# Half of layer 1's query tiles computed in the front, two score places, conditioning sums in PSUM

## The chip, the cores and the metric

The kernel runs on one core of one Trainium2 chip. A core has TensorE (matmuls; "PE" in the profile, and "PEld" for its weight loads), VectorE (DVE), ScalarE (ACT), GpSimd (POOL) and SyncE (SP), which run side by side and wait for one another by semaphores. Data lies in SBUF (on chip), in PSUM (eight banks of 512 fp32 numbers a partition, which matmuls write) and in device memory, which DMA queues read and write; SP's queue and POOL's queue are used here. The metric is the time of one execution on the device in microseconds (us), as the median of several runs.

## What is computed

One inference step of a two-layer trunk. 512 sample tokens and 128 prompt tokens, 640 columns in all, go through the same weights with a model width of 2048, all in fp32. Each layer is: norm, a shift and scale from the conditioning vector, one wide input projection, two mixers with SiLU gates, one output projection, a gated residual. Layer 0 has windowed attention and a short convolution. Layer 1, which is changed here, has differential attention (C) and grouped attention (D):

```python
def odd_mixer(h, w_in, w_out, ...):
    cq, ck, cv, cg, dq, dk, dv, dg = split_cols(h @ w_in, ODD_SPLIT)
    cq = rms_norm(cq..., cqn);  ck = rms_norm(ck..., ckn)
    q_d = rms_norm(q_heads(dq, ...), dqn);  k_d = rms_norm(kv_heads(dk, ...), dkn)
    # samples: rotary on q and k, cached keys and values in front
    o1 = attend(cq[:, 0], ck_all[:, 0], cv_all);  o2 = attend(cq[:, 1], ck_all[:, 1], cv_all)
    o_c = rms_norm(o1 - lam * o2, c_on) * (1 - lam_init)
    y = concat(o_c * silu(cg), attend(q_d, dk_all, dv_all) * silu(dg))
    return y @ w_out
```

C has four heads with two query tiles each (one for each softmax map), D has eight heads that share two keys and are worked on in pairs. So there are 16 query tiles of 128 columns each, eight attention items (four pairs of D, four heads of C), and 52 column tiles in layer 1's input projection. The conditioning of a layer is a product of two vectors with a 2048 x 6144 matrix, in twelve blocks of 512 columns.

## The kernel before

**Numbers.** An fp32 matmul is made of three: weight and data are each split into a rounded part (ACT, line 297) and a rest (VectorE, line 298), and hi x hi, hi x lo and lo x hi are summed in PSUM. The 640 columns are taken in two halves of 320.

**Single tiles and pairs.** A column tile alone (`proj_q`, lines 325 to 334) takes 16 row blocks x 3 products x 2 halves, 96 matmuls of 320 columns. `run_pairs` (lines 534 to 645) takes two column tiles at once by a seven-product scheme in place of eight: 7 x 8 row blocks x 3 = 168 matmuls. It pays with sums on VectorE (lines 566 to 579) and after the products (lines 603 to 609), and it wants the whole of its results at once, in halves, tile by tile; the results go to the function that belongs to the tile (gate, key or value), which ends with a store to device memory.

**Stages** (by the first matmul of each, from the trace): layer 0's single tiles from 36 us, its pairs from 656, its output projection from 880; layer 1's front from 1092 with six single tiles, its 14 pairs from 1180 to 1546 (eight gates, ten keys, ten values); the odd stage from 1546, which has 18 single tiles (16 queries, two gates) with both attentions between them; layer 1's output projection from 2016, its pairs from 2114 to the end.

**The odd stage.** `run_tiles` goes through the tiles in quarters of 24 matmuls. Query tiles 0 and 1 of an item are neighbours; each goes through `q_gen` (line 742: scale and square out of PSUM, a rotary turn with a copy from SBUF to SBUF by DMA, sums of squares, splits). With the second one the item's attention is put into the list `attn`. After each half of a quarter `pace_attn` takes a number of steps of that list, 0.5 to 1 by `steps(i)`. An item has some 14 steps; a full query block of 128 tokens takes two of them (`pair_gen`, line 864; `diff_gen`, line 1554). A step computes scores into PSUM (`scores`, lines 840 to 852), takes the maximum (VectorE, line 808), the exponential (ACT, line 815), transposes the weights (PE, line 834), splits them and weighs the values (lines 897 to 899, 1605 to 1607). Scores have one place of two banks (`pS`), the single tiles have two places (`pproj`, tags pa0, pb0, pa1, pb1), and two banks (`pT`) serve transposes and the rest.

**Fills.** Conditioning blocks that are not needed yet are summed by VectorE, two operations of 512 columns for each of 16 row blocks, in between. `slot` takes steps of such a fill at a given rate. The last four blocks, 8 to 11 of layer 1 (`fill1`, `ada_on_dve`, line 192), are summed in SBUF during the odd stage, fetched by SP's queue, from the third tile on at a rate of 1.1.

**Order.** The program text sets a first order, and the framework orders each engine's instructions by it when it builds, by its own estimate of when each can start; in the trace, scores of the next step can stand amid a weighing. Each engine then works through its list in order. A tile name with `bufs=n` has n buffers, and a new one waits for the oldest to come free.

## Time and profile before

| what | before |
|---|---|
| median of 3 runs | 2251.61 us (2249.99 to 2255.14) |
| the profiled execution | 2249.84 us |
| its span, first to last instruction | 2248.0 us |
| mean granted TensorE clock | 0.998 |
| layer 1's pairs in the front, 1179.7 to 1546.3 | 366.6 us: PE busy 362.8, DVE 255.2, ACT 204.7, POOL 40.6 |
| odd stage up to 2030 | 483.7 us: PE busy 476.3, DVE 370.5, ACT 305.5, POOL 53.8 |

The profile is of one execution. "Busy" is the time in which an engine works on at least one instruction; matmuls overlap, so that a matmul is shown with some 0.31 us while the next one starts 0.15 us after it. A row of a group of instructions gives line, engine, operation, output<-inputs, shapes and count, then busy time and mean ns of one, then the idle time of the engine just before and what ended it. A timeline row begins with the start and the length. A row of waits says which engine at which line waited for which, with total, times and longest.

### The profile page before, as it was taken

To read this page: it belongs to the slowest core of one execution; us is meant where nothing else is said; L and a number is where in the kernel's file an instruction comes from. 1 tells how busy PE (TensorE), PEld (TensorE's weight loads), DVE (VectorE), ACT (ScalarE), POOL (GpSimd) and SP (SyncE) were. 2 spreads that over 40 slices of the span, in tenths; PEclk is the share of its full clock that TensorE was granted. 3 is DMA by queue.
4 is the path that set the end of the run, shared out by engine and by line. 5 is a ranking of instruction groups with operands and counts; after the bars stand their busy time and mean duration, and the time that the engine had idled before them with its cause. 6 is when DMAs were issued, how large, how long until landed. Compare 5 with 4: busy or idle time off the path is not lost.

```text
span 2248.0 us, 41180 instructions
## 1 busy us (share of the span) xinstructions
PE 2208.3 (98%) x15564; PEld 2133.0 (95%) x15564; DVE 1729.8 (77%) x3027; ACT 1131.9 (50%) x2423; POOL 230.1 (10%) x349
## 2 busy tenths in 40 slices
PE   7999999999999999999999999999999999999999
PEld 5889999999999999999999999999999998999999
DVE  5659898989888978877777677765859697976765
ACT  4335453535334445444644466545666666563443
POOL 2211001000100100000100011101000011111010
PEclk9999999999999999999999999999999999999999
DMA  9985556565444526743773333335425343556541
GB/s 357 342 281 180 173 163 209 174 195 171 146 149 122 156 88 198 228 144 121 239 227 114 108 99 105 107 121 163 131 81 162 96 144 113 162 158 228 177 133 44
DMA packets 383543, 365.84 MB, mean 163 GB/s; under 512 B 18786, under 2 KB 326464, under 8 KB 382832
## 3 DMA queue, kind: packets, MB, share of 16 engines
q1 hardware_dynamic: 365984, 300.25, 43.8%
q0 software_dynamic: 16496, 60.74, 7.5%
q8 instruction: 122, 2.00, 0.4%
q10 hardware_dynamic: 864, 2.23, 0.3%
q14 instruction: 77, 0.63, 0.1%
HBM read 310.05 MB, written 46.79 MB: 159 GB/s over the span
## 4 chain that ended last, share of the span: by engine, by line
PE 83%; DMA 5%; issue 4%; DVE 4%; ACT 3%; POOL 2%; SPq 0%; ACTq 0%; POOLq 0%; DVEq 0%
PE pq L627 11%; PE pq L628 11%; PE pq L629 11%; PE pa L332 6%; PE pa L333 6%; PE pb L332 6%; PE pa L334 6%; PE pb L333 6%; PE pb L334 6%; PE T L834 2%; PE S L846 2%; PE S L848 1%; PE S L847 1%; PE T L178 1%; PE T L897 1%
## 5 line engine op out<-in xcount | busy, mean ns | idle before, releaser
L297 ACT ACTIVATE wh<-raw 128x512 fp32r<-128x512 f32 (+1 forms) x364 | 218.5, 601 | 351.8 <-PE pb L333 229.1
L627 PE MATMUL pq<-h,wh 128*128 128x320 f32 x1088 | 338.1, 311 | 0.0
L628 PE MATMUL pq<-h,wh 128*128 128x320 f32 x1088 | 336.2, 309 | 0.0
L629 PE MATMUL pq<-h,wl 128*128 128x320 f32 x1088 | 335.9, 309 | 0.0
L332 PE MATMUL pa<-h,wh 128*128 128x320 f32 x1024 | 325.7, 318 | 0.2 <-DVE sum L426 0.2
L332 PE MATMUL pb<-h,wh 128*128 128x320 f32 x1024 | 321.0, 314 | 0.9 <-ACT h L297 0.9
L333 PE MATMUL pa<-h,wh 128*128 128x320 f32 x1024 | 319.2, 312 | 0.6 <-DVE h L298 0.6
L334 PE MATMUL pb<-h,wl 128*128 128x320 f32 x1024 | 318.5, 311 | 0.2 <-DVE wl L298 0.2
L333 PE MATMUL pb<-h,wh 128*128 128x320 f32 x1024 | 317.7, 310 | 0.0
L334 PE MATMUL pa<-h,wl 128*128 128x320 f32 x1024 | 317.4, 310 | 0.0
L298 DVE TENSOR_TENSOR wl<-raw,wh 128x512 fp32r<-128x512 f32 (+1 forms) x364 | 236.9, 652 | 92.0 <-ACT wh L297 87.9
L627 PE MATMUL pq<-T,wh 128*128 128x320 f32 x816 | 253.8, 311 | 0.0
L629 PE MATMUL pq<-T,wl 128*128 128x320 f32 x816 | 252.3, 309 | 0.1
L628 PE MATMUL pq<-T,wh 128*128 128x320 f32 x816 | 252.0, 309 | 0.0
L297 ACT ACTIVATE wh<-sx 128x512 fp32r<-128x512 f32 x204 | 127.9, 632 | 162.7 <-PE pq L628 117.6
L627 PEld LDWEIGHTS pq<-h,wh 128*128 128x128 f32 x1088 | 204.3, 188 | 0.8 <-issue 0.8
L628 PEld LDWEIGHTS pq<-h,wh 128*128 128x128 f32 x1088 | 204.4, 188 | 0.0
L332 PEld LDWEIGHTS pa<-h,wh 128*128 128x128 f32 x1024 | 192.4, 188 | 12.5 <-issue 11.6
L629 PEld LDWEIGHTS pq<-h,wl 128*128 128x128 f32 x1088 | 204.2, 188 | 0.0
L333 PEld LDWEIGHTS pa<-h,wh 128*128 128x128 f32 x1024 | 192.6, 188 | 6.0 <-issue 4.9
L332 PEld LDWEIGHTS pb<-h,wh 128*128 128x128 f32 x1024 | 193.1, 189 | 2.1 <-ACT h L297 1.1
L334 PEld LDWEIGHTS pa<-h,wl 128*128 128x128 f32 x1024 | 192.4, 188 | 1.6 <-issue 1.6
(399 smaller groups left out, 4904.5 us busy)
## 6 DMA issues: line engine op xcount, KB each, us to landing
adaw<-in_ada_w SPq DMA_DIRECT2D x80, 512.0 KB, 4.0
raw<-in_ev_w_in SPq DMA_DIRECT2D x130, 256.0 KB, 3.3
raw<-in_od_w_in SPq DMA_DIRECT2D x124, 256.0 KB, 3.3
ada<-in_ada_w SPq DMA_DIRECT2D x11, 2048.0 KB, 13.5
w<-in_od_w_in SPq DMA_DIRECT2D x42, 512.0 KB, 3.8
adaw<-in_ada_w SPq DMA_DIRECT2D x64, 256.0 KB, 2.8
w<-in_ev_w_in SPq DMA_DIRECT2D x27, 512.0 KB, 3.7
adah<-in_ada_w SPq DMA_DIRECT2D x20, 512.0 KB, 9.3
```

The lines of the kernel that those rows point to most:

```text
L178: PE.matmul(acc[32 * g:32 * g + 32, 0:wd], sT[:, kt, :], w[:, kt % m, :], start=(i < 4), stop=(i >= KT - 4), tile_position=(0, 32 * g))
L297: A.activation(hi, x, AF.Copy)
L298: V.tensor_sub(lo, x, hi)
L332: PE.matmul(ps, wh[:, i, :], hi[:, sl], start=(j == js[0] if alone else (pos == 0 and j == 0)), stop=False)
L333: PE.matmul(ps, wh[:, i, :], lo[:, sl], start=False, stop=False)
L334: PE.matmul(ps, wl[:, i, :], hi[:, sl], start=False, stop=(j == js[1] - 1 if alone else (pos == 3 and j == 3)))
L627: PE.matmul(ps, wh[:, j, :], hi, start=(first and h == 0 and j == 0), stop=False, skip_group_check=True)
L628: PE.matmul(ps, wh[:, j, :], lo, start=False, stop=False, skip_group_check=True)
L629: PE.matmul(ps, wl[:, j, :], hi, start=False, stop=(final and h == 1 and j == 3), skip_group_check=True)
L834: PE.transpose(t[:, i * P:(i + 1) * P], p, ident)
L846: PE.matmul(d, q[0][:, bs], k[0][:, ks], start=True, stop=False)
L847: PE.matmul(d, q[0][:, bs], k[1][:, ks], start=False, stop=False)
```

## The change

**Queries in the front.** The second query tile of each item (odd heads of D, the second map's tiles of C) leaves the odd stage. These eight columns stand between the keys and the values of the front, as four more pairs. Their results are copied raw to SBUF (`query_out`, buffers "xr") and stored in eight new scratch tiles `qdram` by POOL's queue. In the odd stage `q_rider` loads such a tile and its four turned pieces by SP's queue and does the rest of `q_gen`'s work from SBUF, with the gain put into the rotary operations, together with the item's first query.

**The odd stage** has ten single tiles in place of 18. `steps` is 3.1 and then 3.6 a quarter tile, taken in four parts of six matmuls, and one further step after each tile. All single tiles but the first use one PSUM place (`single`); the other place's two banks (the new pool "more") are closed and serve as a second place for scores (pool "twice"), and the two are taken in turn. Before the output projection they change back; it takes its leads from places 0 and 2.

**Conditioning.** Blocks 8 to 10 move to the front pairs: VectorE sums them in the score place of PSUM, idle there, fetched by POOL's queue into "xr" buffers. `front_rests` sets the rate: for each of two slots of a product, gates 1 at three products of seven, keys 0.5 at three, queries and values 1 at four. Block 11 is summed in the odd stage's first tiles, in buffers "P" of the softmax weights, and is finished before the first attention item begins.

**Smaller parts.** The keys' chain keeps its squares in the mask's buffer, no longer needed, in place of the score place, and stores from its first buffer; the odd stage's "rp" has three buffers for two, "kk" two for one; the heads' key and value loads are grouped a little differently.

```diff
-FILL1 = 1.1
-FILL1_FROM = 8
+FILL1 = 2.2
+    def score_place():
+        if ("twice", "at") not in pools:
+            return pS.tile([P, 1024], F32, tag="S", name="S")
+        st["turn"] = not st.get("turn")
+        return (pS if st["turn"] else pools["twice", "at"]).tile([P, 1024], F32, tag="S", name="S")
...
-    def ada_on_dve(blocks):
+    def ada_in_psum(blocks):
         for l, cb in blocks:
+            both = pS.tile([P, 1024], F32, tag="S", name="adaS")
+            acc = both[:, 0:512], both[:, 512:1024]
+            fetch = lambda kt: ada_in(xr_tile("adaw")[:, 0:512], l, cb, kt, nc.gpsimd)
+            ws = [fetch(0), fetch(1)]
+            yield
+            for kt in range(KT):
+                for _ in ada_rows(l, cb, kt, ws[0], acc):
+                    yield
...
+            acc = [xr_tile(f"acc{c}")[:, 0:512] for c in range(2)]
             for c in range(2):
+                A.copy(acc[c], both[:, c * 512:(c + 1) * 512])
...
+            ada_fold(l, cb, acc, pools["cur"], "xr", 5)
...
+                elif single:
+                    for k in range(4):
+                        proj_q(pp, parts[t], qd, qd, HV[k // 2:k // 2 + 1], js=(k % 2 * 2, k % 2 * 2 + 2), base=0)
+                        if k < 3:
+                            pace_attn(steps(i) / 4)
...
+            if single:
+                pace_attn(1.0)
...
+    def q_rider(j, tag, gain, then=None):
+        ap, (g, turned) = pools["cur"], gain
+        x = ap.tile([P, NT], F32, tag="x2", name="x2", bufs=1)
+        nc.sync.dma_start(x, qdram[j])
+        sw = ap.tile([P, NS], F32, tag="rp", name="qsw", bufs=st["rp"])
+        for d in range(4):
+            nc.sync.dma_start(sw[32 * d:32 * d + 32, :], qdram[j][32 * (d ^ 1):32 * (d ^ 1) + 32, 0:NS])
+        yield
+        sq = ap.tile([P, NT], F32, tag="stg", name="qsq", bufs=2)
+        A.activation(sq, x, AF.Square)
+        m = ap.tile([P, NS], F32, tag="rp", name="qm", bufs=st["rp"])
+        V.scalar_tensor_tensor(out=m, in0=x[:, 0:NS], scalar=g, in1=cosT, op0=ALU.mult, op1=ALU.mult)
+        V.scalar_tensor_tensor(out=sw, in0=sw, scalar=turned, in1=sinT, op0=ALU.mult, op1=ALU.mult)
+        sb = q_sums(ap, sq)
+        yield
...
     def scores(q, blk, k, segs, masks=()):
-        s = pS.tile([P, 1024], F32, tag="S", name="S")
+        s = score_place()
...
+    FRONT_COLS += [OD["dq"] + i * P for i in (1, 3, 5, 7)] + [OD["cq"] + i * P for i in (4, 5, 6, 7)]
+    FRONT_OUT += [(query_out, j) for j in range(8)]
...
+    def front_rests(p, name):
+        out = FRONT_OUT[N_FRONT + 2 * p][0]
+        if out is key_out:
+            return {"M6": 0.5, "M2": 0.5, "M4": 0.5}.get(name, 0.0)
+        return {"M6": 1.0, "M2": 1.0, "M3": 1.0, "M4": 0.0 if out is gate_out else 1.0}.get(name, 0.0)
...
     close("mid")
+    close_psum("more")
+    open_psum("twice")
     open_pool("odd")
-    st["sets"], st["rp"] = 2, 2
+    st["sets"], st["rp"] = 2, 3
+    fill1 = ada_in_rows(1, 11)
...
-    run_tiles(jobs, I["od_w_in"][0], None, fill1, FILL1, fill_from=FILL1_FROM,
-              steps=lambda i: brisk.get(i, 1.0))
+    run_tiles(jobs, I["od_w_in"][0], None, fill1, FILL1, steps=lambda i: 3.1 if i < 6 else 3.6,
+              single=lambda i: 0 if i else 2)
     drain(prep)
+    wait_for("scores", done0 + 8)
```

227 lines of the change are left out of this document (144 added, 83 removed).

## The prediction

> **What bounds the kernel now.** I read the page first: the share of each engine and the chain that ended last.
>
> ```profile
> span 2248.0 us, 41180 instructions
> PE 2208.3 (98%) x15564; PEld 2133.0 (95%) x15564; DVE 1729.8 (77%) x3027; ACT 1131.9 (50%) x2423; POOL 230.1 (10%) x349
> PE 83%; DMA 5%; issue 4%; DVE 4%; ACT 3%; POOL 2%; SPq 0%; ACTq 0%; POOLq 0%; DVEq 0%
> ```
>
> TensorE is busy for 98% of the span and makes up 83% of the chain. A busy row can hide small holes, since matmuls overlap in it, so I take matmul time from the distance of starts instead. Then I asked for the busy times by stretch. The columns are length, PE, PEld, DVE, ACT, POOL, granted clock, DMA share, GB/s.
>
> ```profile
> 730.00:880.00 150.00, 149.95 (x1026) 149.08 (x1025) 127.27 (x200) 68.91 (x121) 8.35 (x16) 1.00 0.42 128
> 1085.00:1090.00 5.00, 3.04 (x23) 2.64 (x22) 3.10 (x10) 2.66 (x6) 2.35 (x3) 1.00 0.94 333
> 1090.00:1096.00 6.00, 5.12 (x21) 4.93 (x21) 4.73 (x12) 4.80 (x14) 0.60 (x1) 0.50 0.82 282
> 1179.70:1546.30 366.60, 362.82 (x2499) 360.13 (x2498) 255.17 (x390) 204.70 (x490) 40.60 (x66) 1.00 0.35 107
> 1546.30:2030.00 483.70, 476.34 (x3334) 451.03 (x3333) 370.46 (x700) 305.54 (x691) 53.83 (x72) 1.00 0.46 139
> 1900.00:2000.00 100.00, 97.41 (x679) 92.13 (x679) 86.29 (x168) 63.31 (x156) 15.77 (x26) 1.00 0.54 163
> ```
>
> The fourth row is layer 1's front pairs, the fifth the odd stage (projections and both attentions). TensorE bounds both; VectorE has 70% and 77% of them, ScalarE 56% and 63%. Two matmuls of a pair, 55 starts apart, give the price of one 320-column matmul:
>
> ```profile
> 1535.80 0.31 PE L628 MATMUL pq<-T,wh 128*128 128x320 f32 x1
> 1543.87 0.31 PE L629 MATMUL pq<-T,wl 128*128 128x320 f32 x1
> ```
>
> 8.07 / 55 = 0.1467 us.
>
> **The change, part by part.** (1) *Eight columns of queries go from single tiles to four pairs.* A single tile is 16 row blocks x 3 products x 2 halves = 96 matmuls; a pair is 7 products x 8 x 3 = 168. Eight tiles cost 768, four pairs 672. The odd stage loses 768 x 0.1467 = 112.7 us of matmuls, the front gains 98.6 us. On the bounding engine that is 96 x 0.1467 = **-14.1 us**, all on the path as long as TensorE stays the bound in both stretches. The rest is about whether it does.
>
> (2) *The front.* What VectorE does for a pair, and what it pays for conditioning, is in the groups of instructions of the stretches 1179.7 to 1546.3 (rows one to five) and 1546.3 to 2030 (the last two):
>
> ```profile
> L298 DVE TENSOR_TENSOR wl<-sx,wh 128x512 fp32r<-128x512 f32 x83 | 56.9, 691 | 37.5 <-ACT wh L297 36.7
> L569 DVE TENSOR_TENSOR sx<-sx,w 128x1024 f32<-128x1024 f32 x14 | 17.1, 1223 | 0.3
> L566 DVE TENSOR_TENSOR sx<-w,raw 128x512 f32<-128x512 f32 x26 | 16.8, 687 | 0.3
> L609 DVE TENSOR_TENSOR tables<-pq,tables 128x320 f32<-128x320 f32 x14 | 6.9, 492 | 7.0 <-PE pq L629 7.0
> L298 DVE TENSOR_TENSOR h<-w,h 128x320 fp32r<-128x320 f32 x8 | 3.6, 487 | 0.0
> L211 DVE SCALAR_TENSOR_TENSOR acc<-adaw,sT,acc 128x512 f32<-128x512 f32 x120 | 86.1, 744 | 6.9 <-DMA adaw<-in_ada_w 6.8
> L298 DVE TENSOR_TENSOR wl<-raw,wh 128x512 fp32r<-128x512 f32 x75 | 51.6, 688 | 31.0 <-ACT wh L297 29.1 <-PE T L899 1.4
> ```
>
> A pair needs 14 splits (14 x 0.691 = 9.7), three sums of 1024 columns and two of 512 (3 x 1.223 + 2 x 0.687 = 5.0) and three of 320 (1.5): 16.2 us beside 168 x 0.1467 = 24.6 us of matmuls. Three conditioning blocks are 3 x 32 = 96 further operations of about 0.744 us, 71 us. The front becomes 366.6 + 98.6 = 465 us with 255 + 4 x 16.2 + 71 = 391 us of VectorE, 84%. Layer 0's pairs, which already carry such fills, show 127.27 of 150 us (85%) with TensorE at 149.95: no stall at that load. The only new thing is that the sums lie in PSUM, which VectorE now writes and no row shows it writing. A read from there costs 0.492 against 0.487 us (rows four and five); I take 0.75, and the ends are 0.744 (no dearer than now) and twice that. The fetches also move from SP's queue to POOL's: 48 issues, queued ahead of the keys' small powers. POOL is busy 40.6 of 366.6 us, so they fit; between nothing and the 3.8 us that TensorE is not busy in the front today (366.60 - 362.82), doubled. The stores of raw queries (eight, also POOL) and two ACT copies a tile have the same cover; the copies replace work that ACT did in the odd stage. I take +1 us, ends 0 and +4; dear PSUM writes are a rival.
>
> (3) *The second score place.* Today the next scores wait until the exponential has read the one place. That is the largest named wait of TensorE in the odd stage, first at the weight load, then at the matmul itself:
>
> ```profile
> PEld S L846 <- ACT p L815: 8.4, 30, 1.1
> PE S L846 <- ACT p L815: 1.8, 3, 0.8
> ```
>
> The weight load's wait overlaps matmuls still running, so the gain lies between -1.8 and -10.2; I take **-5 us**.
>
> (4) *Less projection beside attention.* This is the dear part. Eight items (four dense pairs, four differential heads) now share eight tiles, where they had sixteen. A stretch with little projection between shows what a step costs today; four score steps from the timeline:
>
> ```profile
> 1999.43 0.44 PE L846 MATMUL S<-k1h,q1h 128*128 128x384 f32 x1
> 2016.04 0.44 PE L846 MATMUL S<-k1h,q1h 128*128 128x384 f32 x1
> ...
> 1996.00:2016.00 20.00, 20.00 (x145) 18.88 (x144) 15.13 (x31) 13.59 (x34) 1.73 (x4) 1.00 0.19 60
> ```
>
> 16.61 / 4 = 4.15 us, and counting the timeline 37 projection matmuls stand between, 9.3 a step. After the change a quarter tile (24 matmuls) is shared by 3.1 or 3.6 steps: 7.7 or 6.7 a step. So the density is a fifth to a quarter beyond one that TensorE got through without a hole. What can open is the way from the transposes over both splits to the weighing:
>
> ```profile
> 1996.72 0.81 PE L834 MATMUL T<-ident,p 128*128 128x128 f32 x6
> 1997.35 0.60 ACT L297 ACTIVATE pth<-T 128x512 fp32r<-128x512 f32 x1
> 1997.98 1.02 DVE L298 TENSOR_TENSOR ptl<-T,pth 128x512 fp32r<-128x512 f32 x2
> 1998.84 0.28 PE L1605 MATMUL T<-vh,pth 128*128 128x256 f32 x1
> ```
>
> Projections start again at 1997.29 and the weighing at 1998.84: 1.55 us to cover, and 6.7 or 7.7 matmuls cover 0.98 or 1.13. Missing are 0.57 or 0.42 us in each of 16 + 16 full query blocks, 15.8 us in all, if nothing else stands there. Something does: in the same place the trace runs the next scores amid the weighing (weighing at 1998.84, scores at 1999.43), and with two places they can come earlier. So the ends are 0 and, where busier ACT and DVE also delay the splits, twice 15.8; I take **+6 us**, nearer to the lower end because the thin stretch above has PE busy 20.00 of 20. The engines themselves have room: VectorE 370 - 71 (three of the four blocks, 96 x 0.744) - 22 (32 splits x 0.688) = 277 of 484 - 113 = 371 us, 75%; it has 86% in 1900 to 2000 today.
>
> (5) *The opening of the odd stage.* Block 11 and four queries, keys and values now fall on the first two tiles, before attention may begin (its P places hold the sums): 32 x 0.744 = 23.8 us of fills, 11 x 0.688 = 7.6 of weight splits, two queries of three rotary operations and a split (4 x 0.686 and 0.3 for the prompt's part, 6 together) and, as an estimate, some 4 for keys and values (five splits of 640 columns or less). That is 41 us of VectorE beside 2 x 14.1 us of matmuls. Attention begins 41 us into the stage today as well, but with a third tile's matmuls before it:
>
> ```profile
> 1587.23 0.34 PE L846 MATMUL S<-k0h,q0h 128*128 128x384 f32 x1
> ...
> L762 DVE TENSOR_TENSOR qsw<-qsw,tables 128x512 f32<-128x512 f32 x16 | 11.0, 686 | 2.9 <-DMA qsw<-qx 2.8
> L298 DVE TENSOR_TENSOR h<-yin,h 128x640 fp32r<-128x640 f32 x12 | 9.7, 816 | 0.4 <-ACT h L297 0.4
> ```
>
> The hole is at most 41 - 28 = 13 us. Three quarters of the third tile (3 x 3.5 us) have their weights ordered by then and can fill it: **+3 us**, ends 0 and 13.
>
> (6) *One PSUM bank for the single tiles.* The next tile's first half waits until ACT has copied and squared it (0.52 + 0.43 us):
>
> ```profile
> L746 ACT ACTIVATE qx<-pa,vec 128x320 f32<-128x320 f32 x16 | 8.4, 524 | 9.7 <-PE pa L334 7.0 <-issue 1.5 <-DMA raw<-in_od_w_in 1.2
> L747 ACT ACTIVATE qsq<-pa 128x320 f32<-128x320 f32 x16 | 7.0, 434 | 0.0
> ```
>
> The second half's last 12 matmuls (1.76 us) and one attention step stand in between. Behind that wait in TensorE's queue is everything, so a late ACT costs in full: 0 to 9 x 1 us, **+2**.
>
> (7) *Riders.* Each rider loads its tile and four turned pieces from DRAM on SP's queue, one issue more than before, a full tile ahead of use; the DMA share is 0.46 and falls with 8 weight columns gone. Nothing, as long as that tile's 14 us cover the load. The output projection's banks change places: nothing.
>
> Sum: -14.1 + 1 - 5 + 6 + 3 + 2 = -7.1 us. The profiled execution took 2249.84 us (span 2248.0 and 1.8 around it), so 2242.7; that execution lies 1.8 below the median of the runs (2251.61), within their spread of 5. I predict **2243 us**.
>
> **The rivals.** *Thin filler (slower).* The covering scores are not there in time, because exponentials and splits queue on ACT and DVE, and every full query block opens a hole between transposes and weighing. Place: the 32 blocks of the odd stage. Price at 0.7 us each: 22 us in place of 6, so 2259. It outweighs the fewer matmuls alone from 14.1 / 32 = 0.44 us a block, and the whole sum from 13 us / 32 = 0.41. For it: 0.42 to 0.57 us are really uncovered by projections; against it: the full 20 us above. Chance 0.25.
> *Everything hides.* No hole opens, the opening is filled, score waits go: 2249.84 - 14.1 - 7 = 2229. Against it: ACT and DVE both rise to some three quarters of the stage with chains between them. Chance 0.15.
> *The front turns VectorE-bound.* At 1.49 us for a sum in PSUM, a query or value pair with eight fills needs 16.2 + 11.9 = 28.1 against 24.6 us: 9 x 3.5 = 31 us, 2274. It decides from (24.6 - 16.2) / 8 = 1.05 us an operation. Against it: 0.492 beside 0.487. Chance 0.08.
> *The opening stays a hole.* 8 us uncovered in place of 3, and the clock falls: after TensorE's gap in 1085 to 1090 the next 6 us were granted 0.50, so 3 us more: 2243 + 8 = 2251, no change. Chance 0.10. [...]
>
> **How the numbers follow.** My forecast (2236 to 2250) has 0.42, the rivals 0.25, 0.15, 0.08 and 0.10. A difference of 0.2% (4.5 us) is about what a measurement of this kernel can tell. Faster is most of my own case (0.38) and all of "everything hides": 0.53. Within 0.2%: the rest of mine, most of the opening and the mild part of thin filler: 0.18. Slower: 0.29. The range 2230 to 2264 leaves out the dear PSUM sums, the worst of thin filler and half of "everything hides", under 0.2 together.
>
> **What would show it.** Matmuls of the pair lines in the front up by 672, single ones down by 768 (1). Front near 465 us with PE busy within 5 us of it, and a fill in PSUM near 0.75 us (2). No wait of scores for the exponential (3). The odd stage's span: 371 us plus or minus few; waits of weighing or transposes for splits above 13 us in total mean thin filler (4). First scores near 41 us into the stage with TensorE holes before (5). Waits of single tiles' matmuls for ACT's square (6). I am wrong if VectorE or ACT, not TensorE, ends most waits of the odd stage, or if TensorE pauses in the front.

## The result

The changed kernel takes 2270.97 us (median of 6 runs, 2262.72 to 2276.05), the kernel before on the same chip 2252.56 (6 runs). The ratio is 1.008, with a 95% interval of 1.0067 to 1.0092: 0.8% slower, where 2243 and a range of 2230 to 2264 had been forecast. The profiled execution took 2271.45 us, 21.6 more than that of the kernel before.

The page of the changed kernel, with the span, the engines' shares and the chain that ended last:

```profile
span 2269.7 us, 41141 instructions
PE 2204.6 (97%) x15468; PEld 2118.8 (93%) x15468; DVE 1765.4 (78%) x3075; ACT 1147.2 (51%) x2457; POOL 258.3 (11%) x413
PE 79%; DVE 5%; issue 5%; DMA 5%; ACT 4%; POOL 2%; SPq 1%; POOLq 0%; DVEq 0%; ACTq 0%
```

TensorE issues 96 instructions fewer (15468 against 15564) and holds four points less of the chain, while the span grew. To see where, I cut at the first matmul of a stage. The first row is the changed kernel's front pairs, the second its odd stage with the output projection's single tiles; the columns are length, PE, PEld, DVE, ACT, POOL, granted clock, DMA share, GB/s.

```profile
1184.20:1651.40 467.20, 464.12 (x3200) 459.81 (x3200) 375.66 (x583) 253.49 (x583) 70.09 (x122) 1.00 0.43 134
1651.40:2135.50 484.10, 451.81 (x3099) 417.86 (x3098) 339.75 (x653) 303.51 (x688) 57.61 (x87) 1.00 0.45 139
```

And the second of these stretches in the kernel before:

```profile
1546.30:2113.80 567.50, 558.21 (x3897) 532.21 (x3896) 424.22 (x798) 336.52 (x747) 63.37 (x88) 1.00 0.49 151
```

With the front row that the prediction shows (366.6 us), the two stretches took 366.6 + 567.5 = 934.1 us before and 467.2 + 484.1 = 951.3 after: 17.2 more. The other 4.5 of the span's 21.7 lie ahead of the front pairs (they begin at 1184.2, before at 1179.7), in stages that the change doesn't touch; the medians differ by 18.4, so I take 17.2 as the change's own. With 96 matmuls fewer, at the prediction's 0.1467 us each, the two stretches should have taken 920.0, so 31 us were lost.

A measure that serves for all runs below is the *rest* of the odd stage: its length less its single-tile matmuls at 0.1467 us. Before: 567.5 - 2304 x 0.1467 = 229.5 us. After: 484.1 - 1536 x 0.1467 = 258.8. The rest holds the attention's own matmuls, which are the same in both, and TensorE's holes. It grew by 29.3 us. Most of that stands in the rows: TensorE is not busy for 484.1 - 451.8 = 32.3 us, before for 9.3, so 23.0 of the 29.3 are open holes; the other 6.3 lie in stretches that count as busy. The front's excess over its matmuls is 467.2 - (366.6 + 98.6) = 2.0 us. So all but 2.0 us of the loss is in the odd stage.

### The profile page after: what moved, and what is told of

The parts are those of the page before. It is cut to its first block, busy times and chain, and to the rows that moved or that the text cites. A ratio compares the mean times of both kernels' runs of the same rounds, so it can differ in the third digit from the quotient of the medians.

```text
span 2269.7 us, 41141 instructions
## 1 busy us (share of the span) xinstructions
PE 2204.6 (97%) x15468; PEld 2118.8 (93%) x15468; DVE 1765.4 (78%) x3075; ACT 1147.2 (51%) x2457; POOL 258.3 (11%) x413
## 4 chain that ended last, share of the span: by engine, by line
PE 79%; DVE 5%; issue 5%; DMA 5%; ACT 4%; POOL 2%; SPq 1%; POOLq 0%; DVEq 0%; ACTq 0%
PE pq L676 12%; PE pq L677 12%; PE pq L678 12%; PE pa L373 5%; PE pa L374 5%; PE pa L375 5%; PE pb L373 5%; PE pb L375 4%; PE pb L374 4%; PE T L914 2%; PE T L196 1%; PE S L926 1%; DMA ada<-in_ada_w 1%; PE S L927 1%; PE S L928 1%
## 5 line engine op out<-in xcount | busy, mean ns | idle before, releaser
L676 PE MATMUL pq<-h,wh 128*128 128x320 f32 x1216 | 377.9, 311 | 0.0
L677 PE MATMUL pq<-h,wh 128*128 128x320 f32 x1216 | 375.9, 309 | 0.0
L676 PE MATMUL pq<-T,wh 128*128 128x320 f32 x912 | 283.6, 311 | 0.0
L677 PE MATMUL pq<-T,wh 128*128 128x320 f32 x912 | 281.8, 309 | 0.0
L373 PE MATMUL pa<-h,wh 128*128 128x320 f32 x880 | 280.0, 318 | 1.1 <-ACT qsq L796 0.9
L373 PE MATMUL pb<-h,wh 128*128 128x320 f32 x880 | 276.4, 315 | 1.2 <-ACT h L337 0.9
L374 PE MATMUL pa<-h,wh 128*128 128x320 f32 x880 | 275.9, 314 | 1.0 <-DVE h L338 1.0
L375 PE MATMUL pb<-h,wl 128*128 128x320 f32 x880 | 274.8, 312 | 0.8 <-DVE wl L338 0.8
L374 PE MATMUL pb<-h,wh 128*128 128x320 f32 x880 | 274.1, 312 | 0.0
L676 PEld LDWEIGHTS pq<-h,wh 128*128 128x128 f32 x1216 | 228.3, 188 | 1.6 <-issue 1.6
L677 PEld LDWEIGHTS pq<-h,wh 128*128 128x128 f32 x1216 | 228.4, 188 | 0.0
L338 DVE TENSOR_TENSOR wl<-sx,wh 128x512 fp32r<-128x512 f32 x228 | 156.2, 689 | 49.6 <-ACT wh L337 44.4
L291 DVE SCALAR_TENSOR_TENSOR acc<-adaw,sT,acc 128x1024 f32<-128x1024 f32 x150 | 189.6, 1277 | 0.0
L373 PEld LDWEIGHTS pa<-h,wh 128*128 128x128 f32 x880 | 166.0, 189 | 12.6 <-issue 10.1
L676 PEld LDWEIGHTS pq<-T,wh 128*128 128x128 f32 x912 | 171.5, 188 | 0.4 <-issue 0.4
```

Source lines behind the costliest of these rows:

```text
L291: V.scalar_tensor_tensor(out=acc[c], in0=w, scalar=sT[:, kt, c:c + 1], in1=acc[c], op0=ALU.mult, op1=ALU.add)
L338: V.tensor_sub(lo, x, hi)
L373: PE.matmul(ps, wh[:, i, :], hi[:, sl], start=(j == js[0] if alone else (pos == 0 and j == 0)), stop=False)
L374: PE.matmul(ps, wh[:, i, :], lo[:, sl], start=False, stop=False)
L375: PE.matmul(ps, wl[:, i, :], hi[:, sl], start=False, stop=(j == js[1] - 1 if alone else (pos == 3 and j == 3)))
L676: PE.matmul(ps, wh[:, j, :], hi, start=(first and h == 0 and j == 0), stop=False, skip_group_check=True)
```

## Where the odd stage loses: the opening

The timeline of the changed kernel from the first scores of the odd stage to its first exponential:

```profile
1683.83 0.44 PE L926 MATMUL S<-k0h,q0h 128*128 128x384 f32 x1 [1.08 <-ACT q0h L337]
...
1704.60 1.42 DVE L214 SCALAR_TENSOR_TENSOR adap<-adap,sT 128x512 f32<-128x512 f32 x2 [0.18 <-DMA adap<-in_ada_w]
...
1708.85 1.00 ACT L895 ACTIVATE p<-S,nm,rq 128x768 f32<-128x768 f32 x1
```

The first scores come 32 us into the stage, and their exponential 25 us later. In between VectorE adds up block 11 (`adap`, L214), in the four "P" places that the exponential writes to; its last sum begins at 1705.3. The description of the change has block 11 finished before the first attention item begins; on the chip it isn't, the first scores run ahead of its end by some 22 us. The same stretch by short windows, and the wait behind its largest hole:

```profile
1684.00:1709.00 25.00, 20.30 (x115) 17.72 (x116) 21.18 (x33) 5.75 (x15) 2.21 (x1) 0.93 0.76 234
1709.00:1735.00 26.00, 21.72 (x142) 18.30 (x141) 20.29 (x42) 25.39 (x53) 0.00 (x0) 1.00 0.25 74
...
1696.00:1700.00 4.00, 2.21 (x16) 1.95 (x14) 3.85 (x7) 0.59 (x2) 0.00 (x0) 1.00 0.57 174
1700.00:1704.00 4.00, 2.66 (x10) 2.66 (x11) 4.00 (x8) 0.40 (x1) 0.00 (x0) 0.66 0.68 195
```
```profile
PEld pa L375 <- DVE wl L338: 3.4, 1, 3.4
```

ScalarE is busy for 5.75 of 25 us, and its first exponential begins only at the end of them. VectorE is busy for 21.18, and a weight split late in its queue stops even the projections for 3.4 us, after which the granted clock is 0.66 over 1700 to 1704. Then everything held back comes at once: in the next 26 us ScalarE is busy for 25.39, and TensorE still for only 21.72.

## Where the odd stage loses: waits of the output transposes

From the waits of the changed kernel's odd stage (who waits at which line for whom; total, times, longest), the largest rows that concern scores, weighing (L977 to L979, L1686 to L1688) and the heads' output; the second fence has the output transposes in the same stage of the kernel before:

```profile
ACT on L1690 <- PE T L1688: 25.3, 16, 3.4
DVE on L1700 <- POOL rn L1696: 21.3, 17, 3.9
PEld S L926 <- ACT p L895: 7.8, 15, 1.5
PEld T L1705 <- DVE ptl L338: 5.9, 9, 1.0
PE T L1705 <- DVE on L1700: 5.2, 7, 0.8
PE S L926 <- ACT p L895: 3.9, 4, 1.3
PE T L1705 <- DVE ptl L338: 3.4, 7, 0.8
PEld T L977 <- ACT pth L337: 2.8, 8, 0.9
PEld T L978 <- DVE ptl L338: 1.7, 3, 0.9
PEld T L977 <- DVE ptl L338: 1.5, 4, 0.8
PEld pa L373 <- ACT qsq L796: 1.2, 1, 1.2
PEld T L1686 <- DVE ptl L338: 0.9, 3, 0.4
```
```profile
PEld T L1624 <- DVE on L1619: 2.1, 3, 1.0
PE T L1624 <- DVE on L1619: 1.6, 4, 0.7
```

A differential head's output of one query block goes through four engines and back to the first: weighing on TensorE (L1686 to L1688), scaling on ScalarE (L1690), the normalisation's sum on POOL (L1694, L1696), the scaling by it on VectorE (L1700), the transposes on TensorE (L1705). With all of their rows together, smaller ones than these included, these transposes are the weight load's most waited-for place: 14.6 us at L1705, where it was 4.1 at L1624 before. The weighing, where the prediction had looked for the hole, has 6.9 us in the four rows above. The transposes wait for two things. In seven of their waits the scaling `on` ends the wait of the load or of the matmul behind it (7.0 us at the load): that is the chain. In nine it is `ptl`, the split of the next block's probabilities (5.9 us): by the program the transposes write one of only two places "T", and this split is the last reader of theirs.

## The experiments

All ratios are to the kernel before on the same chip; the medians come from several chips, on which that kernel took 2250.23 to 2252.56 us. "Front" is the length of the front pairs, "odd" that of the odd stage with the output's single tiles, both cut as above, "rest" as above; 2304, 1920 or 1536 single-tile matmuls are taken off. These three come from one profiled execution of each kernel, which lies up to 3.7 us from the kernel's median (e3: 2253.30), so differences of 2 or 3 us say little.

| kernel | median us | ratio to before (95%) | front | odd | rest |
|---|---|---|---|---|---|
| before | 2252.56 | 1 | 366.6 | 567.5 | 229.5 |
| after | 2270.97 | 1.008 (1.0067 to 1.0092) | 467.2 | 484.1 | 258.8 |
| e1 block 11 in the front too | 2257.98 | 1.0034 (1.0023 to 1.0046) | 470.0 | 471.8 | 246.5 |
| e2 output transposes later | 2261.25 | 1.0041 (1.0027 to 1.0056) | 467.3 | 478.0 | 252.7 |
| e3 both of these | 2249.64 | 0.9993 (0.9981 to 1.0004) | 470.0 | 464.2 | 238.9 |
| e4 one score place | 2296.47 | 1.0203 (1.0188 to 1.0219) | 467.4 | 510.4 | 285.1 |
| e5 only D's queries moved | 2254.01 | 1.0009 (1.0 to 1.0019) | 428.8 | 508.3 | 226.6 |
| e6 only C's queries moved | 2254.79 | 1.0011 (1.0001 to 1.002) | 429.1 | 508.6 | 226.9 |
| e7 conditioning alone | 2249.27 | 0.9987 (0.9978 to 0.9997) | 371.0 | 561.2 | 223.2 |
| e8 before, outputs later | 2255.63 | 1.0014 (1.0004 to 1.0023) | 366.6 | 571.5 | 233.5 |
| e9 as e5, fills done in the front | 2241.22 | 0.9951 (0.9933 to 0.997) | 419.6 | 505.4 | 223.7 |
| e10 as e3, weighing later | 2252.14 | 1.0002 (0.9989 to 1.0014) | 470.0 | 465.1 | 239.8 |
| e11 places of its own for block 11 | 2266.89 | 1.0067 (1.0051 to 1.0082) | 467.3 | 483.2 | 257.9 |
| e12 as e6, fills done in the front | 2245.53 | 0.9968 (0.9958 to 0.9978) | 419.7 | 507.9 | 226.2 |

The same rest, cut once more, at the end of the last weighing of a dense item and of the last output transposes of a head. The last column is the time of the stage in which the trace grants a clock of 0.50. There a projection matmul starts 0.27 us after the one before it (1702 us in the changed kernel), not 0.15, so some half of this time is lost (an estimate).

| kernel | opening and dense items | four heads | remainder | us at clock 0.50 |
|---|---|---|---|---|
| before | 116.1 | 108.1 | 5.4 | 0 |
| after | 135.4 | 117.3 | 6.2 | 3.4 |
| e1 | 118.8 | 118.3 | 9.4 | 3.4 |
| e2 | 134.3 | 111.6 | 7.1 | 10.2 |
| e3 | 119.5 | 111.6 | 7.8 | 6.8 |
| e4 | 136.7 | 142.2 | 6.4 | 34.1 |
| e7 | 113.0 | 104.9 | 5.3 | 0 |
| e9 | 113.1 | 101.2 | 9.4 | 3.4 |
| e11 | 129.5 | 118.4 | 10.0 | 13.7 |
| e12 | 108.7 | 110.8 | 6.7 | 0 |

**Block 11, the output transposes, and both (e1, e2, e3).** The first moves block 11 to the front, too; the second issues a block's output half a unit later than its scores.

```diff
-    fill1 = ada_in_psum([(1, cb) for cb in range(8, 11)])
+    fill1 = ada_in_psum([(1, cb) for cb in range(8, 12)])
...
-            return {"M6": 0.5, "M2": 0.5, "M4": 0.5}.get(name, 0.0)
-        return {"M6": 1.0, "M2": 1.0, "M3": 1.0, "M4": 0.0 if out is gate_out else 1.0}.get(name, 0.0)
+            return {"M6": 1.0, "M2": 1.0, "M4": 1.0}.get(name, 0.0)
+        return {"M6": 1.0, "M2": 1.0, "M3": 1.0, "M4": 0.0 if out is gate_out else 1.0,
+                "M7": 1.0 if out is gate_out else 0.5}.get(name, 0.0)
...
-    fill1 = ada_in_rows(1, 11)
+    fill1 = iter(())
```
```diff
-            if u >= 3:
-                out(u - 3)
+            if u == 7:
+                out(4)
             if 2 <= u < 7:
                 weigh(u - 2)
...
             if u < 5:
                 score(u, 1)
+            if u >= 3:
+                out(u - 3)
```

> Edit to the changed kernel: block 11 is summed in the front's pairs too, so the odd stage's first tiles carry no fill and the P places are free from the start. Theory A (the opening): in the changed kernel the first exponential waits 25 us after the first scores (1683.8 to 1708.9) because block 11's sums hold all four P places and VectorE works through them until 1706; TensorE loses some 16 us more than before in the first two items. Without the fill the odd stage shortens by 12 to 18 us: 2253 to 2259 us. Theory B (thin filler everywhere): the opening is only where the missing projection shows first, and the holes move to the next items; the gain is below 5 us: 2266 or more. Against both: if the front cannot take a fourth block (VectorE at 89% of it), the front's 467 us grow.

> Edit to the changed kernel: in a differential head the transposes of a finished block's output are issued half a unit (one step) later. Theory A2 (one late chain): weighing, ACT's scale and square, POOL's two operations and VectorE's scaling take longer than the step that now lies before the transposes; TensorE stands some 13 us before line 1705 in the four heads, and a step's delay takes 8 to 13 us off: 2258 to 2263 us. Theory B (thin filler everywhere): TensorE then waits at the next operation, below 3 us: 2268 or more.

> Both edits, block 11 in the front and the outputs one step later. If the two places are the whole of the loss, their gains add, 20 to 30 us: 2241 to 2251 us, at or below the kernel before. By thin filler in general: above 2262.

The rest fell by 12.3 us in e1, by 6.1 in e2 and by 19.9 in e3 (258.8 to 238.9). The two causes are separate, e1's gain lies in the opening and the dense items and e2's mainly in the heads, and they add up: with half of the time at clock 0.50 taken off, the three gains are 12.3, 9.5 and 21.6 us. e2 delays the transposes past both of their waits, the chain and the place "T", so it doesn't tell these two apart. The front paid 2.8 us for block 11. In e3 the opening has no hole; its timeline and windows:

```profile
1683.32 0.34 PE L926 MATMUL S<-k0h,q0h 128*128 128x384 f32 x1
...
1685.95 0.99 ACT L895 ACTIVATE p<-S,nm,rq 128x768 f32<-128x768 f32 x1
```
```profile
1684.00:1709.00 25.00, 25.00 (x171) 23.48 (x170) 18.28 (x32) 21.12 (x45) 0.00 (x0) 1.00 0.27 80
1709.00:1735.00 26.00, 25.92 (x183) 23.84 (x183) 14.87 (x30) 19.80 (x46) 3.84 (x4) 1.00 0.21 66
```

The exponential follows the first scores by 2.6 us, and TensorE is busy throughout. Even so e3 only breaks even with the kernel before: its rest is still 9.4 us above that one's, some 3.4 of it by the clock.

**One score place (e4).**

```diff
     def score_place():
-        if ("twice", "at") not in pools:
+        if True:
             return pS.tile([P, 1024], F32, tag="S", name="S")
```

> Edit to the changed kernel: scores always take the first place, the second one stays unused; all else as changed. It prices the second place by itself, the term that the prediction put at -5 us (between 1.8 and 10). If score chains of 3.8 to 4.2 us a step bound the heads without it, the steps (some 2.7 us on average, 3.6 to 3.9 in full blocks) cannot keep up and the kernel gets 10 to 25 us slower: 2281 to 2296. If the scores' waits were hidden by projections in any case, within 5 us: 2266 to 2276.

The odd stage takes 26.3 us longer, at the upper end of what was expected. Two rows of its waits answer to those of the changed kernel (7.8 and 3.9), and the third line is the window of its odd stage:

```profile
PEld S L926 <- ACT p L895: 17.6, 25, 3.4
PE S L926 <- ACT p L895: 11.2, 7, 3.2
1651.70:2162.10 510.40, 469.24 (x3098) 429.64 (x3098) 347.24 (x653) 305.21 (x688) 59.31 (x87) 0.97 0.43 132
```

So the second place is worth some 26 us in this stage, and more than half of that is the clock, by an estimate: it is granted at 0.50 for 34.1 us here and for 3.4 in the changed kernel, and half of the difference is some 15 of the 26 us. TensorE is not busy for 41.2 us of the stage, where it was 32.3 in the changed kernel: 8.9 us more of open holes. What the place would be worth beside the full filler wasn't tried.

**Half of the change, and the conditioning alone (e5, e6, e7, e8).** e5 and e6 start from e3 and move only one half of the queries: D's (the second tiles of the four dense items) or C's (those of the four heads); the other half stays single tiles. The steps of attention a quarter tile are set to go with it: 1.7 beside the heads in e5, 1.6 beside the dense items in e6. e7 starts from the kernel before and adds only the PSUM sums of blocks 8 to 10, in its 14 front pairs (with the keys' chain as changed), with block 11 left in the odd stage. e8 is the kernel before with the later output of e2.

A part of e5's edit:

```diff
-    FRONT_COLS += [OD["dq"] + i * P for i in (1, 3, 5, 7)] + [OD["cq"] + i * P for i in (4, 5, 6, 7)]
-    FRONT_OUT += [(query_out, j) for j in range(8)]
+    FRONT_COLS += [OD["dq"] + i * P for i in (1, 3, 5, 7)]
+    FRONT_OUT += [(query_out, j) for j in range(4)]
...
-    jobs += [(OD["cq"] + h * P, with_rest("c_q_norm", head_rest, h, done0 + 4 + h)) for h in range(4)]
+    for h in range(4):
+        jobs.append((OD["cq"] + h * P, q_job("q0", "c_q_norm")))
+        jobs.append((OD["cq"] + (4 + h) * P, last_q(h)))
```

> Half of the move, on top of both edits (all four blocks in the front, outputs one step later): only D's four second queries join the front (two pairs more than before), C's second queries stay single tiles of the odd stage. 48 matmuls fewer than before, -7.0 us. With both edits and all eight queries moved, TensorE's holes in the four dense items were 16 us as in the kernel before, those of the four heads 27 in place of 18. Theory C (pairs of D bear thin filler, heads of C do not): the holes are as before everywhere, 2240 to 2246 us, faster than both kernels. Theory B (every item pays about 1.7 us for thin filler): the four thin items take back the 7 us, 2248 to 2253.

> The other half, same edits: only C's four second queries join the front, D's stay single tiles. Also 48 matmuls fewer than before. Theory C: the heads lose 9 us to holes against 7 gained: 2250 to 2256 us. Theory B: as with D's half, 2248 to 2253; the pair of runs tells by its difference, 8 to 10 us by C and under 3 by B.

> The kernel before with one part of the change alone: blocks 8 to 10 are summed in PSUM during the front's 14 pairs (with the keys' chain as changed, since it needs the score place otherwise), block 11 stays in the odd stage as it was; no query moves, one score place, two places for single tiles. If TensorE bounds both stages, as read before the change, relief of VectorE by 71 us in the odd stage is worth 0 to 4 us: 2246 to 2251. If VectorE's load had set the odd stage, 10 us or more: below 2241. If sums in PSUM are dear, the front's 366.6 us grow: above 2255.

> The kernel before with the one edit of the outputs one step later. With some 12 projection matmuls a step the chain over ACT, POOL and VectorE was covered, so nothing is to be gained: 2248 to 2253 us. If it gains 4 us or more, the late chain was there before the change and did not come from thin filler.

e5 and e6 came out alike in time, though one leaves the heads full and the other thin; both lie above the range of theory B, and theory C's difference of 8 to 10 us is not there. Their rests (226.6 and 226.9) are below that of the kernel before; what they lost is in the front, 428.8 and 429.1 us where its matmuls need 366.6 + 2 x 24.6 = 415.9. With only 16 pairs the conditioning doesn't finish there, and what is left is run at the end of the front with TensorE waiting. A row of the waits of e5 there, and its windows:

```profile
PE T L262 <- ACT acc L238: 6.6, 1, 6.6
```
```profile
1600.00:1604.00 4.00, 1.37 (x10) 0.87 (x8) 2.11 (x3) 1.70 (x4) 2.15 (x5) 0.92 1.03 341
1604.00:1608.00 4.00, 0.00 (x0) 0.00 (x0) 1.26 (x2) 0.00 (x0) 0.35 (x1) 0.50 0.92 299
1608.00:1612.00 4.00, 3.08 (x14) 1.93 (x15) 0.47 (x3) 2.08 (x4) 0.00 (x0) 0.50 0.80 310
```

This hole is of the experiment's own making, so e9 and e12 below repeat the two halves without it. e7 shows what the conditioning is worth by itself: the rest falls by 6.3 us, the front takes 4.4 more, and 1.9 stay. e8's stage got 4.0 us longer (and the kernel slower than the range given): with full filler a later output is no gain in itself. It mends only what the thin filler uncovers.

**The weighing later (e10).** In e3 the weighing does wait for the splits, as the prediction had it. The first fence is from e3's waits in the four heads, 1857 to 2024.1 us; the second from e10's, 1851 to 2021.4.

```diff
         for u in range(8):
-            if u == 7:
-                out(4)
-            if 2 <= u < 7:
-                weigh(u - 2)
+            if u >= 3:
+                norm(u - 3)
             if u < 5:
                 score(u, 0)
             if u == 7:
+                out(4)
                 break
             yield
+            if u >= 3:
+                out(u - 3)
             if u >= 2:
-                norm(u - 2)
+                weigh(u - 2)
             if u < 5:
                 score(u, 1)
-            if u >= 3:
-                out(u - 3)
```

> The kernel of e3 (block 11 also in the front, output transposes half a unit later), and in the differential heads the weighing of a tile is issued in the second half of a unit, its normalisation at the head of the next one's first half. Theory of the prediction's fourth term (the thin filler leaves holes between the probability transposes and the weighing): the holes of the four heads fall by 4 to 10 us together, the time is 2240 to 2246 us. Rival (the holes are where the filler is short of the chain from scores over exponential to transposes, wherever the weighing stands): they move to the scores or the transposes, and the time is within 3 us of e3, 2247 to 2252 us.

```profile
PEld T L1686 <- DVE ptl L338: 5.4, 10, 0.8
PE T L1705 <- DVE on L1700: 2.5, 4, 0.7
PEld S L926 <- ACT p L895: 0.9, 3, 0.4
```
```profile
PE T L1705 <- DVE on L1700: 6.6, 7, 2.1
PEld S L926 <- ACT p L895: 2.9, 5, 1.5
PEld T L1686 <- DVE ptl L338: 0.4, 1, 0.4
```

The weighing's wait went from 5.4 to 0.4 us and came back at the output transposes and the scores. The rest stayed (238.9, 239.8), and the ratio, 1.0002, lies within the interval of e3's. The weighing's place is not what costs.

**Places of its own for block 11 (e11).**

```diff
-        place = lambda: ap.tile([P, 768], F32, tag="P", name="adap", bufs=P_BUFS)[:, 0:512]
-        acc = place(), place()
+        tags = ["vh", "vl"]
+
+        def place():
+            tags.reverse()
+            return ap.tile([P, 512], F32, tag=tags[0], name="adap")
+        both = ap.tile([P, 2, NT], F32, tag="y", name="adac", bufs=1)
+        acc = both[:, 0, 0:512], both[:, 1, 0:512]
...
-            ada_fold(l, cb, acc, ap, "P", P_BUFS)
+            ada_fold(l, cb, acc, ap, "on", 2)
```

> The changed kernel with one thing moved: the odd stage's conditioning of block 11 adds up in a tile of its own and reads weights from buffers of their own, so that the four places of the probability tiles are free when the attention opens; VectorE does the same additions as in the changed kernel. Theory P (the opening's hole is the first exponential that waits for a probability place held by block 11): the first exponential follows the first scores within 5 us, and the time is 6 to 10 us below the changed kernel's, 2261 to 2265 us. Rival V (the opening is late because VectorE is loaded with block 11's additions, whatever tiles they use): within 3 us of the changed kernel, 2268 to 2274 us.

The first exponential indeed comes earlier, though not within the 5 us of theory P; TensorE stays busy in the first window, but not in the second (timeline, then windows of e11; its lines stand five lower in the file):

```profile
1682.11 0.69 PE L931 MATMUL S<-k0h,q0h 128*128 128x384 f32 x1 [2.64 <-ACT q0h L342]
...
1689.78 0.99 ACT L900 ACTIVATE p<-S,nm,rq 128x768 f32<-128x768 f32 x1
```
```profile
1684.00:1709.00 25.00, 24.99 (x152) 23.50 (x152) 21.47 (x38) 14.35 (x30) 0.00 (x0) 0.92 0.70 211
1709.00:1735.00 26.00, 21.43 (x148) 17.90 (x148) 22.45 (x45) 22.11 (x51) 1.60 (x1) 1.00 0.27 77
```

The exponential is 7.7 us behind the first scores in place of 25. Over the two windows TensorE is not busy for 4.6 us, where it was 9.0 in the changed kernel and 0.1 in e3: so about half of the opening's hole was theory P's wait for a place, and the other half, left with VectorE loaded as before, fits rival V. VectorE is busy for 21.47 and 22.45 us of the two windows, where in e3 it needs 18.28 and 14.87. Still the stage takes 483.2 us, against 484.1. Of the 5.9 us that the opening and the dense items gained, 4.9 went again in the heads and the remainder. The clock has a part in this: TensorE pauses for 2.64 us ahead of the first scores (timeline above), and from 1681.37 us on the granted clock is 0.50 for 6.82 us:

```profile
1677.96:1681.37 3.41, 1.51 (x11) 1.25 (x9) 3.40 (x7) 0.00 (x0) 1.90 (x1) 1.00 0.63 183
1681.37:1688.19 6.82, 6.08 (x21) 6.08 (x22) 5.29 (x9) 2.94 (x7) 0.00 (x0) 0.50 0.76 238
```

In all, 13.7 us of this stage were at 0.50, against 3.4 in the changed kernel; half of the difference, some 5 us, is an estimate of what that costs. The median (2266.89) lies between the two expectations, and its interval overlaps that of the changed kernel. Nor is the edit clean: its buffers are those of the values (`vh`, `vl`), whose split begins at 1704.0 us here and at 1688.7 or before in the changed kernel. So neither theory holds alone: the places and VectorE's time for block 11 both take part in the opening's price, and how the whole 12.3 us divide between them stays open.

**Each half with the conditioning finished in the front (e9, e12).** Higher rates in the front; e9 also has the outputs in their original place.

```diff
-            return {"M6": 1.0, "M2": 1.0, "M4": 1.0, "M7": 0.5}.get(name, 0.0)
+            return {"M6": 1.0, "M2": 1.0, "M4": 1.0, "M7": 1.0}.get(name, 0.0)
...
-                "M7": 1.0}.get(name, 0.0)
+                "M7": 1.0, "M5": 0.5}.get(name, 0.0)
```

> The kernel of e5 (only the four second queries of the query tile D's items are projected in the front, C's stay single tiles beside the attention), with the output transposes in their original place and with higher rates in the front, so that the conditioning of all four blocks is finished before the front ends. Theory B (each query tile taken out of the attention's filler costs about as much in thin filler as its pairing saves): what was left in e5 above the kernel before is the drained rest at the end of the front, one hole of about 7 us; without it 2243 to 2247 us, and the front pairs take 414 to 418 us. Rival: VectorE, now above 90 per cent busy in the front, sets its pace; then the front pairs take over 420 us and the time is 2250 to 2256 us.

> The kernel of e6 (only the second queries of the four heads are projected in the front, the query tile D's stay single tiles beside the attention's start; output transposes half a unit later) with the higher rates of e9 in the front, and nothing else, so that the conditioning is finished before the front ends. Theory B (either half alone leaves enough filler for the attention, and only both together run it thin): as e9, the hole at the front's end goes, front pairs 418 to 423 us, time 2243 to 2248 us. Rival H (it is the four heads, whose five weighings of two score tiles each need the fill, that run thin, whatever stands beside the dense items): the heads keep their holes of some 6 us each, and the time is 2249 to 2256 us.

Both halves are faster than the kernel before, e9 by 0.5% (2241.22 us, the fastest kernel of this study, and faster than theory B's range for it), e12 by 0.3%. The front takes 419.6 and 419.7 us, 3.7 above its matmuls; VectorE is busy for 361.88 of e9's 419.60 us there (86%), and TensorE is not busy for only 2.9:

```profile
1182.30:1601.90 419.60, 416.69 (x2875) 410.82 (x2874) 361.88 (x574) 230.94 (x544) 76.42 (x134) 1.00 0.48 146
```

By their whole rests the halves look nearly free: 223.2 us in e7, which has all the filler, 223.7 in e9, 226.2 in e12, and 238.9 in e3 with both halves moved. But e7 is no like baseline. It has one score place and still sums block 11 in the odd stage, while e9, e12 and e3 have two places and all the conditioning in the front; e12 and e3 have the later outputs, e9 hasn't. The table by stretches compares like with like. The four heads have a rest of 101.2 us with full filler (e9; 102.9 in e5, with the later outputs), of 110.8 with thin filler beside full dense items (e12), and of 111.6 with thin filler throughout (e3). So thin heads cost some 8 to 10 us whether or not the other half has been moved. Their rows, e9 first, then e12, then e3:

```profile
1807.60:2014.00 206.40, 203.51 (x1437) 195.57 (x1436) 144.85 (x286) 134.80 (x336) 32.26 (x56) 1.00 0.37 112
```
```profile
1844.90:2016.90 172.00, 164.30 (x1149) 152.03 (x1147) 134.27 (x273) 123.31 (x314) 33.50 (x57) 1.00 0.39 119
```
```profile
1856.60:2024.10 167.50, 157.78 (x1094) 144.49 (x1092) 131.31 (x270) 120.81 (x307) 28.52 (x55) 1.00 0.37 114
```

TensorE is not busy for 2.9 us in e9, for 7.7 in e12 and for 9.7 in e3. No engine beside TensorE is full: VectorE and ScalarE have 78% and 72% of e3's row, 70% and 65% of e9's. Rival H of e12 named the right stretch, though the holes are some 2 us a head, not 6, and the time came out as by theory B. For the opening and the dense items the rest is 108.7 us with full filler (e12), 113.1 (e9) and 119.5 (e3) with thin.

Taking the lower figures together, 108.7 + 101.2 + 6.7 = 216.6 us is an estimate of the rest with nothing thin, two score places and all the conditioning in the front. No run has this. Against it D's half costs 7.1 us, C's half 9.6 and both 22.3; with half of the time at clock 0.50 taken off, 5.4, 9.6 and 18.9. Each half saves 7.0 us of matmuls. So it isn't shown that the price grows faster than the number of tiles taken away, nor that the halves gain by their queries: by this estimate D's half about breaks even, C's loses, and what made e9 and e12 faster is largely the rest of the change.

## Why the prediction was wrong

(1) *The matmuls.* Right. The whole profile's counts of pair and single matmuls moved by 672 and 768: the groups of instructions of the whole span show it, after first, with 1216 + 912 pair matmuls on each of three lines, before with 1088 + 816. (The third row belongs to the next point.)

```profile
L676 PE MATMUL pq<-h,wh 128*128 128x320 f32 x1216 | 377.9, 311 | 0.0
L676 PE MATMUL pq<-T,wh 128*128 128x320 f32 x912 | 283.6, 311 | 0.0
L214 DVE SCALAR_TENSOR_TENSOR adaS<-adaw,sT,adaS 128x512 f32<-128x512 f32 x90 | 67.5, 750 | 3.6 <-DMA adaw<-in_ada_w 3.3
```
```profile
L627 PE MATMUL pq<-h,wh 128*128 128x320 f32 x1088 | 338.1, 311 | 0.0
L627 PE MATMUL pq<-T,wh 128*128 128x320 f32 x816 | 253.8, 311 | 0.0
```

That is 224 more on each of three lines. The 14.1 us were saved, and lost again elsewhere.

(2) *The front.* Right: 467.2 us for 465 + 1, a sum in PSUM 750 ns for 0.75 us (third row), and VectorE not the bound. The rival of dear PSUM sums falls.

(3) *The second score place.* Wrong: the wait that it was to remove stayed. The scores' waits for the exponential did not go; they are 7.8 and 3.9 us, where they had been 8.4 and 1.8. The place is worth 26 us within the changed kernel (e4), but against the kernel before no gain of 5 us shows. A wait that is taken away in a stage whose filler is taken away as well isn't a gain that can be added. What the place gains with full filler no run shows.

(4) *Less projection beside attention.* This is the step that failed, in place and in size. Terms (3) to (6) together were to add 6 us to the rest of the stage; they added 29.3. The price was worked out from one place, the way from the splits to the weighing. The sign given for it ("above 13 us in total") was just missed: 6.9 us for the weighing, and 5.9 for output transposes that wait for a split, which the prediction hadn't meant. It had left out the heads' output transposes, which wait for a chain from TensorE through ScalarE, POOL and VectorE back to TensorE, and for a place "T". The full filler covers most of this (4.1 us of waits at the load before, and e8: delaying them there only costs), the thin one doesn't (14.6 us of waits; 6.1 us of the rest by e2). The rows of the kernel before had the chain in them, small as it was. With that and block 11 mended, the stage still lost 9.4 us against the kernel before, and e10 shows that it isn't the weighing's place. The stretch that I had trusted, 20 us in the heads with PE busy 20.00, has 9.3 matmuls a step; the heads of e12 and e3 have 3.6 steps to 24 matmuls, 6.7 a step, and TensorE is not busy for 7.7 and 9.7 us there. So the reading didn't carry over from 9.3 to 6.7. Of the rivals, *thin filler* (2259) had the side right, not the place.

(5) *The opening.* Wrong in place, undersized, the other large part. First scores were expected 41 us into the stage with a hole ahead of them; they came at 32 us, and most of the hole is behind them. Block 11's sums cost 12.3 us in the stage, 9.5 with what they cost in the front (e1), in place of 3. The prediction did list the 23.8 us of VectorE, and that the "P" places hold the sums, but it set them only against the start of the attention, not against the exponentials and splits that follow it. The rival with a hole and half clock had a part of it: the hole of 3.4 us ends within 1700 to 1704, and the granted clock over these 4 us is 0.66. In the changed kernel that is small: 0.93 over 25 us are 1.8 us. The runs have a lower clock with pauses of several kinds: the 3.4 us here, 0.50 in and behind e5's hole of 6.6 us, and in e11 0.50 behind 3.41 us in which TensorE was busy for 1.51. How long or how empty a pause must be for it, they don't show.

(6) *One bank for single tiles.* Near enough, 1.2 us at the weight load (`qsq` row) for 2. (7) *Riders.* No wait of TensorE for their loads is among the rows of the stage; ScalarE waits for one once (2.5 us). They weren't tested alone.

The sum, by the runs: -14.1 for the matmuls, +2.0 in the front, +29.3 in the rest, 17.2 us slower. The rest's 29.3 are 12.3 for block 11, 6.1 for the output transposes, 1.5 that the two gain together beyond their sum, and 9.4 that stayed in e3. The clock moves these by up to 3.4 us.

What stays open: which single wait of the heads ends the thin filler's cover, what share of the output transposes' price is the chain and what the place "T", and what the queries' halves are worth by themselves, for which a kernel with two score places, all four blocks in the front and every query in the odd stage is missing. The holes that are left in e3's heads are many and short (5.4 us over ten waits is the largest row), and moving one (e10) only moved them.

## What to carry to other kernels

Filler that hides chains on other engines has a price: here some 8 to 10 us in the four heads, for tiles whose pairing saves 7.0. Cost it by the density that the stage will have, not by a stretch that ran well at a higher one, and list every wait that the filler still covers, the small ones too: the output transposes stood with 2.1 and 1.6 us in the waits of the kernel before. Compare a part of a change with a kernel that differs in that part alone; here the halves looked free beside a baseline that lacked other parts of the change. Where a change saves work by taking filler away, try half of it all the same: the half was 0.5% faster than the kernel before, and the whole 0.8% slower.

## What was not expected of the hardware

VectorE's sums cost hardly more in PSUM than in SBUF: 750 ns (third row of the first fence under "Why the prediction was wrong") against 744 for the same operation in SBUF before. And VectorE at 86% of a stretch left TensorE idle for only 2.9 of 419.6 us in e9's front, while at 85% (21.18 of 25 us) in the changed kernel's opening, with a weight split, queries and sums in one queue, it stopped TensorE for 3.4 us at once. The busy share alone did not tell the two apart. Nor was so much time at a low clock expected: with one score place (e4) 34.1 us of the odd stage ran at 0.50, against 3.4 in the changed kernel, and in e11 the 0.50 came behind 3.41 us in which TensorE still worked for 1.51.
